# S5's gated result: from a way through DRAM to products of 64x64 blocks with the identity

## The chip, the core and the metric

The kernel runs on one core of one Trainium2 chip. The metric is the device time of one execution in microseconds (us), the median of several runs. TensorE is called PE in the profile, its weight loads PEld, VectorE DVE, ScalarE ACT, GpSimd POOL and SyncE SP. DMA transfers are started from the queues of SP, ACT and POOL.

## What is computed

A layer of an encoder on 512 tokens of 1024 channels, in float32. What matters here is the S5 branch. From the 512 columns `xa` of a projection, seen as 32 groups of 16 channels, it runs a linear recurrence over the tokens forwards and backwards, adds a skip, and passes the sum through gelu. The result y (512 tokens x 512 channels) is multiplied by the sigmoid of its own product with `w_glu`:

```
y = d.reshape(32, 16) * u                      # u: xa as (tokens, 1, 32 groups, 16 channels)
for direction, reverse in ((0, False), (1, True)):
    y = y + s5_scan(u, ..., reverse)
y = gelu(y.reshape(1, tokens, 512))
y = y * sigmoid(y @ w_glu)
```

Beside it runs a gMLP branch. Both are projected (`w_proj_a`, `w_proj_b`), gated, summed and projected by `w_out`; then follow attention over 256 memory tokens and a SwiGLU feed-forward part with a last norm.

## The kernel before, in words

**Large products.** Each float32 weight block is loaded by SP (`wraw`), split into a high part by ScalarE (`whi`, line 85) and a low part by VectorE (`wlo`, line 86), and multiplied in three products of halves (`mm3`, line 350). `feat` gives results with channels on partitions, `tokm` with tokens on partitions. `next_w` keeps the blocks coming: loads are begun three blocks ahead and splits are made two ahead. After each block `tick` runs; it counts time in units of 5.2 us (one `feat` block of 24 products at full width) and calls what was put off by `later(n, fn)` to n such units on. So S5's small steps are laid between the large products.

**Order.** The program is traced in the order of the code, and the library then orders each engine's instructions by a simulated timeline. An instruction may move ahead of others on its engine when its inputs come early. `in_order` (`tc.keep_in_program_order`) pins an instruction behind the one traced last on its engine.

**S5's time axis.** The 512 tokens are 64 chunks (`NCH`) of 8 positions (`Q`). The 32 groups are worked on in four octets (`NO` = 4, `GO` = 8). For octet o, `s5_outputs` does this:

- `ss` is copied out of the states (lines 952, 953).
- `mix_` makes, in one PSUM bank `py`, 24 products of 64 weight columns and 128 moving columns (line 966), in two halves of the array: partitions 0 to 63 and 64 to 127 are the 64 chunks, once for each of two groups, and the free axis is 4 pairs x (8 positions x 16 channels).
- `squash`, at the next tick, applies gelu on ScalarE (line 972) into the first half of the tile `tt`, seen as `yt[:, 0]`.
- `back`, one unit of time after that, turns the four 128x128 blocks by PE transposes into the bank `pyt` (line 978). They are not pinned. Partitions are then (position, channel), the free axis (group, chunk).
- `emit` copies the bank to the second half of `tt` (line 982), and eight transfers of 32 KB, four from SP's queue and four from ScalarE's, write it to the DRAM tile `yd` (line 986), with channels in front.

The octets' input side (`apply`, line 902) makes 16 products of 64 weight columns and 64 moving columns, in two halves of the array, into the bank `pz`; `keep` copies that (line 907). `pump` calls two of them at a time. `products` (lines 818 and 825, bank `pk`) makes the kernels of the octet after next.

**Merge.** When all of S5 is traced, its pool is closed and the pool `merge` opened. Four loads bring `yd` back as `ygt` (line 1174; 128 channels on partitions, m = 0 to 3, the free axis (position, chunk)); each is split into `yg_hi` and `yg_lo`. Then `feat` multiplies by `w_glu`, and `glu_evac` takes the sigmoid and multiplies by `ygt` (line 1183). `w_proj_a` (with the gates `gat`, line 1196) and `w_out` follow.

**The tag "gain".** The pool `norm` has two slots of 4 KB per partition with this tag. They hold, in turn, `g_mix`, `g_row`, `gbr`, `mix`, `g_mem` (the gain of the memory's norm, used at line 498 on `mt`), `g_x` (used there on `h` into `xs`), two tiles of probabilities, `g_f`, `s3`, `pair` and `g_o`. The gains are loaded from SP's queue (line 460). A tile's load waits until the slot's tenant before it has been read.

Of the kernel before, what the change touches and what calls it, by code (L numbers as in the profile page):

```python
# [9 lines left out]
F32 = mybir.dt.float32  # L10
F32R = mybir.dt.float32r
AF = mybir.ActivationFunctionType
ALU = mybir.AluOpType
# [4 lines left out]
P = 128  # L18
D = 1024
T = 512  # L20
# [7 lines left out]
C = 16  # L28
# [11 lines left out]
Q = 8  # L40
NCH = T // Q
NO = 4
GO = G // NO
# [9 lines left out]
def hybrid_layer_kernel(  # L53
# [8 lines left out]
    nc = tc.nc  # L62
# [8 lines left out]
    np_ = ctx.enter_context(tc.tile_pool(name="norm", bufs=2))  # L71
    dp = ctx.enter_context(tc.tile_pool(name="scratch", bufs=1, space=DRAM))
# [4 lines left out]
    def bank(name):  # L77
        return pm.tile([P, 512], F32, tag="mm", name=name)

    def aux(name, shape=(P, 512)):  # L80
        return pa.tile(list(shape), F32, tag="aux", name=name)

    def split(dst_hi, dst_lo, src):

        hi = nc.scalar.copy(dst_hi, src)  # L85
        lo = nc.vector.tensor_tensor(dst_lo, src, dst_hi.bitcast(F32), ALU.subtract)  # L86
        if pinned[0]:
            in_order(hi)
            in_order(lo)
# [3 lines left out]
    in_order = tc.keep_in_program_order  # L93
# [338 lines left out]
    def later(n, fn):  # L432

        side["later"].append((side["now"] + n, fn))
# [28 lines left out]
    ident = cp.tile([P, P], F32, name="ident")  # L463
# [135 lines left out]


    ud = dp.tile([SW, Q, NCH], F32, name="ud")
    yd = [dp.tile([GO * C, Q, NCH], F32, name=f"yd{o}") for o in range(NO)]
    st = {}
    V = nc.vector
    lo_, hi_ = slice(0, 64), slice(64, 128)
# [174 lines left out]
    def lc(t, g):  # L780
        return t[:, g].rearrange("p a b -> p (a b)")
# [160 lines left out]
    def s5_outputs(o):  # L942
        gs = slice(o * GO, (o + 1) * GO)
        while ("oct", o) not in st:
            yield None
        e_re, e_im, tt = st["oct", o]
        zh, u = st["zh"], st["u"]
        ss = s5p.tile([P, 2, GO, NCH], F32, tag="wt", name="ss", bufs=2)
        zv = zh[:, :, :, gs].rearrange("p n i g -> p i g n")
        nc.gpsimd.memset(ss[lo_, :, :, 0:1], 0.0)  # L950
        nc.gpsimd.memset(ss[hi_, :, :, NCH - 1:NCH], 0.0)
        nc.scalar.copy(ss[lo_, :, :, 1:NCH], zv[lo_, :, :, 0:NCH - 1])
        nc.scalar.copy(ss[hi_, :, :, 0:NCH - 1], zv[hi_, :, :, 0:NCH - 1][:, :, :, ::-1])
        ss = (ss[:, 0], ss[:, 1])

        yt = tt.rearrange("p (i r) c -> p i r c", i=2)

        def mix_():
            ps = aux("py", (P, GO // 2, P))
            for r in range(GO // 2):  # L960
                for k in range(3):
                    for j in range(2):
                        g = 2 * r + j
                        a = (u[:, o * GO + g, :], ss[0][:, g, :], ss[1][:, g, :])[k]
                        b = (tt[:, g, :], lc(e_re, g), lc(e_im, g))[k]
                        in_order(nc.tensor.matmul(ps[64 * j:64 * j + 64, r, :], a, b, start=r == k == 0, stop=k == 2,  # L966
                                                  tile_position=(0, 64 * j), skip_group_check=True))
            later(0.5, lambda: squash(ps))

        def squash(ps):  # L970

            nc.scalar.activation(yt[:, 0], ps, AF.Gelu_apprx_tanh)
            later(1, back)

        def back():
            ps = aux("pyt", (P, GO // 2, P))
            for r in range(GO // 2):
                nc.tensor.transpose(ps[:, r, :], yt[:, 0, r, :], ident)
            later(0.5, lambda: emit(ps))

        def emit(ps):
            nc.scalar.copy(yt[:, 1], ps)
            y = yt[:, 1].rearrange("p r (g n) -> p (r g) n", n=NCH)
            ydo = yd[o].rearrange("(g c) l n -> l c g n", c=C)
            for l in range(Q):
                (nc.sync, nc.scalar)[l % 2].dma_start(ydo[l], y[C * l:C * l + C])

        later(0.5, mix_)
        yield 0.1
        yield None  # L990

    def s5_program():
        yield from s5_setup()
        st["zh"] = s5p.tile([P, NCH, 2, G], F32, name="zh")
        later(0.5, pump)
        for n in range(6):
            yield from s5_input(n)
        yield from s5_kernels(0)
        for n in range(6, len(SETS)):
            yield from s5_input(n)  # L1000
        for _ in range(2):
            square_power()
        yield from s5_kernels(1)
        while st.get("nz", 0) < 2 * NO:
            yield None
        yield None
        yield from s5_scan()
        for _ in range(2):
            yield None
        for o in range(NO):  # L1010
            yield from s5_outputs(o)
            if o + 2 < NO:
                yield from s5_kernels(o + 2)
# [114 lines left out]
    for h in range(H):  # L1128
        ps = bank("psv")
# [36 lines left out]
    mgp = mgx.enter_context(tc.tile_pool(name="merge", bufs=1))  # L1166
# [2 lines left out]

    yg_hi = mgp.tile([P, 4, T], F32R, name="yg_hi")  # L1170
    yg_lo = mgp.tile([P, 4, T], F32R, name="yg_lo")
    ygt = mgp.tile([P, 4, T], F32, name="ygt")
    for m in range(4):
        nc.sync.dma_start(ygt[:, m, :], yd[m].rearrange("p l n -> p (l n)"))
        split(yg_hi[:, m, :], yg_lo[:, m, :], ygt[:, m, :])
    ya_hi = mgp.tile([P, 4, T], F32R, name="ya_hi")
    ya_lo = mgp.tile([P, 4, T], F32R, name="ya_lo")

    def glu_evac(m, j, ps):
        z = np_.tile([P, T], F32, tag="ev", name="glu", bufs=2)  # L1180
        nc.scalar.activation(z, ps, AF.Sigmoid)
        z2 = np_.tile([P, NCH, Q], F32, tag="ev", name="glu2", bufs=2)
        nc.vector.tensor_tensor(z2.rearrange("p n l -> p l n"), z.rearrange("p (l n) -> p l n", l=Q),
                                ygt[:, m, :].rearrange("p (l n) -> p l n", l=Q), ALU.mult)
        split(ya_hi[:, m, :], ya_lo[:, m, :], z2.rearrange("p n l -> p (n l)"))

    for c0 in range(0, SW, 256):
        feat(w_glu, c0, (yg_hi, yg_lo), 4, glu_evac)
# [275 lines left out]
    for t0 in (0, 2):  # L1464
        ps = {t: bank(f"pt{t - t0}") for t in (t0, t0 + 1)}
# [77 lines left out]
    ps = [bank("pf0"), bank("pf1")]  # L1543
# [192 lines left out]
    for i in range(2):  # L1736
        p = aux("pcut", (P, 256))
# [37 lines left out]
```

## Time and profile before

| what | value |
|---|---|
| median of 3 runs | 876.34 us |
| lowest and highest run | 876.28 and 878.51 us |
| the profiled execution | 877.18 us |
| its span, first to last instruction | 875.4 us |
| mean granted TensorE clock | 0.997 |
| DMA packets | 112134 |
| moved by DMA | 154.34 MB, 176 GB/s in the mean |

The span is what the engines' instructions cover in the profiled execution; the execution's own time is a little longer. Busy time of PE counts matmuls whose ends are modelled, and matmuls overlap, so prices on PE are read from start to start. A row of a tile or line view gives the count, the shortest, median and longest instruction in ns, and the first and last start in us. In the order of time a row gives start, length, engine, line, operation, result and operands, the used rows and columns of the weights, the moving size, and the count of what was merged into the row.

### The profile page before, as it was taken

The page shows a single profiled execution, that of the slowest core. Times are in us where ns is not written, and L with a number is a line of the kernel's source. Part 1 is how long each engine was busy: PE and PEld are TensorE (multiplying, and loading weights), DVE is VectorE, ACT ScalarE, POOL GpSimd, SP SyncE. Part 2 cuts the span into 40 slices and gives each one's busy share as a digit, 9 for nine tenths or more (in the row PEclk, how much of TensorE's full clock was granted, in tenths as well). Part 3 has the DMA queues.
Part 4 walks back from the last instruction along what each step waited for, and adds up shares of the span by engine and source line. Part 5 has one row for each costly group of instructions (what it writes and reads, how often), then busy time and mean ns, then how long its engine had stood idle before and what let it go on. Part 6 is the DMA issues. An engine that isn't in the chain of part 4 may idle for free.

```text
span 875.4 us, 14560 instructions
## 1 busy us (share of the span) xinstructions
PE 862.9 (99%) x5753; PEld 759.9 (87%) x5753; DVE 617.4 (71%) x867; ACT 464.1 (53%) x684; POOL 104.9 (12%) x154
## 2 busy tenths in 40 slices
PE   9999999999999999999999999999999999999996
PEld 6787888887888888889899878999999999888875
DVE  5699679968313258669657646767877768898875
ACT  5544875277434234557557444645545454556663
POOL 1001065103311100110000001001111110000000
PEclk9999999999999999999999999999999999999998
DMA  8358369943759946825687144547788963256672
GB/s 260 112 148 249 78 200 257 248 125 107 205 133 278 263 134 211 270 88 174 196 262 218 52 137 128 145 129 187 178 217 212 233 165 79 82 166 198 194 249 87
DMA packets 112134, 154.34 MB, mean 176 GB/s; under 512 B 13545, under 2 KB 78593, under 8 KB 112002
## 3 DMA queue, kind: packets, MB, share of 16 engines
q1 hardware_dynamic: 93042, 128.27, 45.2%
q0 software_dynamic: 16432, 24.09, 16.6%
q10 hardware_dynamic: 2592, 1.05, 0.5%
q8 instruction: 45, 0.74, 0.3%
q14 instruction: 23, 0.19, 0.1%
HBM read 146.60 MB, written 38.24 MB: 211 GB/s over the span
## 4 chain that ended last, share of the span: by engine, by line
PE 93%; DVE 5%; ACT 1%; issue 1%; POOL 0%; POOLq 0%
PE pf L350 29%; PE pt L350 17%; PE px L1370 12%; PE dx L350 7%; PE pq L1370 6%; PE dq L350 3%; PE pv L1370 3%; PE qx L1370 2%; PE dv L350 2%; PE ptr L511 1%; PE py L966 1%; PE po L350 1%; PE qq L1370 1%; DVE wlo L86 1%; PE pz L902 1%; PE pw L883 1%
## 5 line engine op out<-in xcount | busy, mean ns | idle before, releaser
L86 DVE TENSOR_TENSOR wlo<-wraw,whi 128x1024 fp32r<-128x1024 f32 (+1 forms) x139 | 165.0, 1187 | 110.2 <-ACT whi L85 106.9
L85 ACT CAST whi<-wraw 128x1024 fp32r<-128x1024 f32 (+1 forms) x139 | 142.3, 1024 | 168.2 <-PE pf L350 60.1
L350 PE MATMUL pf<-xn,whi 128*128 128x512 f32 x448 | 140.6, 393 | 0.0
L350 PEld LDWEIGHTS pf<-xn,whi 128*128 128x128 f32 x448 | 83.4, 188 | 17.9 <-issue 1.1
L350 PE MATMUL pf<-xn,wlo 128*128 128x512 f32 x224 | 87.7, 391 | 0.0
L1370 PE MATMUL px<-fn,whi 128*128 128x256 f32 x480 | 83.3, 277 | 0.0
L1370 PEld LDWEIGHTS px<-fn,whi 128*128 128x128 f32 x480 | 72.4, 188 | 0.3 <-ACT u L1630 0.2
L85 ACT CAST whi<-b 128x1024 fp32r<-128x1024 f32 x40 | 42.1, 1053 | 50.5 <-PE px L1370 27.1
L86 DVE TENSOR_TENSOR wlo<-b,whi 128x1024 fp32r<-128x1024 f32 x40 | 49.0, 1224 | 28.0 <-ACT whi L85 28.0
L1370 PE MATMUL px<-fn,wlo 128*128 128x256 f32 x240 | 66.5, 277 | 0.0
L350 PE MATMUL dx<-whi,s 128*128 128x512 f32 x170 | 53.9, 392 | 1.4 <-ACT whi L85 1.0
L1370 PE MATMUL pq<-s,whi 128*128 128x256 f32 x320 | 55.1, 277 | 0.0
L86 DVE TENSOR_TENSOR wlo<-t,whi 128x1024 fp32r<-128x1024 f32 x30 | 36.7, 1225 | 20.1 <-ACT whi L85 20.1
L85 ACT CAST whi<-t 128x1024 fp32r<-128x1024 f32 x30 | 31.6, 1052 | 36.0 <-PE pv L1370 12.6
L350 PEld LDWEIGHTS pf<-xn,wlo 128*128 128x128 f32 x224 | 42.1, 188 | 8.6
L1370 PEld LDWEIGHTS pq<-s,whi 128*128 128x128 f32 x320 | 48.3, 188 | 0.1
L1370 PEld LDWEIGHTS px<-fn,wlo 128*128 128x128 f32 x240 | 45.1, 188 | 0.0
L1370 PE MATMUL pq<-s,wlo 128*128 128x256 f32 x160 | 44.3, 277 | 0.0
L350 PE MATMUL pt<-whi,xn 128*128 128x512 f32 x128 | 42.4, 404 | 0.0
L350 PEld LDWEIGHTS dx<-whi,s 128*128 128x128 f32 x170 | 31.7, 188 | 8.4 <-ACT whi L85 1.2
L350 PE MATMUL dx<-wlo,s 128*128 128x512 f32 x85 | 33.1, 390 | 0.0
L1370 PEld LDWEIGHTS pq<-s,wlo 128*128 128x128 f32 x160 | 30.1, 188 | 0.0
(436 smaller groups left out, 2132.1 us busy)
## 6 DMA issues: line engine op xcount, KB each, us to landing
wraw<-in_w_in_dram SPq DMA_DIRECT2D x36, 512.0 KB, 5.2
dsum<-in_w_down_dram SPq DMA_DIRECT2D x20, 512.0 KB, 6.9
wraw<-dsum SPq DMA_DIRECT2D x20, 512.0 KB, 4.1
b<-in_w_gate_dram SPq DMA_DIRECT2D x15, 512.0 KB, 4.1
b<-in_w_up_dram SPq DMA_DIRECT2D x15, 512.0 KB, 3.9
wraw<-in_w_down_dram SPq DMA_DIRECT2D x15, 512.0 KB, 3.8
dsum<-in_w_down_dram POOLq DMA_DIRECT2D x10, 512.0 KB, 7.6
dsum<-dsum POOLq DMA_DIRECT2D x10, 512.0 KB, 7.7
```

Source lines behind the costliest of these rows:

```text
L85: hi = nc.scalar.copy(dst_hi, src)
L86: lo = nc.vector.tensor_tensor(dst_lo, src, dst_hi.bitcast(F32), ALU.subtract)
L350: nc.tensor.matmul(ps, a[x], b[y], start=start and i == 0, stop=stop and i == 2, skip_group_check=free)
L511: tr = nc.tensor.transpose(ps[:, j, :], src[:, k * P:(k + 1) * P], ident)
L883: nc.tensor.transpose(ps[:, j, :], wt[:, 4 * hf + j, :], ident)
L902: in_order(nc.tensor.matmul(ps[hf, g, :], wt[:, g, hf], x, start=g == 0, stop=True, tile_position=(0, 64 * j), skip_group_check=True))
L966: in_order(nc.tensor.matmul(ps[64 * j:64 * j + 64, r, :], a, b, start=r == k == 0, stop=k == 2, tile_position=(0, 64 * j), skip_group_chec ...
L1370: nc.tensor.matmul(ps[:, j, :], a[x], b[y], start=start and j == k == i == 0, stop=k == 3 and i == 2, skip_group_check=True)
```

## The change

`mix_` pairs group 4j + r with half j and place r, in place of group 2r + j, so that each half holds four neighbouring groups. `squash` writes gelu's result to the first half of `tt` in another order: `yl`, with the position in front and then (group, channel). Each of its 64x64 blocks (64 chunks on partitions, 64 channels of one position free) is then turned by an ordinary product with the 64x64 identity, in the quarter of the array that belongs to its half: 16 products an octet, pinned by `in_order`. The bank then has 128 channels on partitions and (position, chunk) free, which is the layout of `ygt`. `emit` copies it to one of two tiles `ygt` in the slots "gain", each for two octets. The DRAM tile `yd`, its 32 writes, the four loads and the tile `ygt` of the pool `merge` go away; the splits and `glu_evac` read the new tiles.

```diff
-    yd = [dp.tile([GO * C, Q, NCH], F32, name=f"yd{o}") for o in range(NO)]
+    ygt = []
...
-        yt = tt.rearrange("p (i r) c -> p i r c", i=2)
+        yl = tt[:, 0:GO // 2, :].rearrange("p r (i c) -> p (r i) c", i=2)
...
-                        g = 2 * r + j
+                        g = GO // 2 * j + r
...
-            nc.scalar.activation(yt[:, 0], ps, AF.Gelu_apprx_tanh)
+            nc.scalar.activation(yl.rearrange("p l (r c) -> p r l c", c=C), ps.rearrange("p r (l c) -> p r l c", c=C),
+                                 AF.Gelu_apprx_tanh)
             later(1, back)
 
         def back():
-            ps = aux("pyt", (P, GO // 2, P))
-            for r in range(GO // 2):
-                nc.tensor.transpose(ps[:, r, :], yt[:, 0, r, :], ident)
+
+            ps = aux("pyt", (P, Q, NCH))
+            for l in range(Q):
+                for j in range(2):
+                    hf = slice(64 * j, 64 * j + 64)
+                    in_order(nc.tensor.matmul(ps[hf, l, :], yl[hf, l, :], ident[hf, hf], start=l == 0, stop=True,
+                                              tile_position=(64 * j, 64 * j), skip_group_check=True))
             later(0.5, lambda: emit(ps))
 
         def emit(ps):
-            nc.scalar.copy(yt[:, 1], ps)
-            y = yt[:, 1].rearrange("p r (g n) -> p (r g) n", n=NCH)
-            ydo = yd[o].rearrange("(g c) l n -> l c g n", c=C)
-            for l in range(Q):
-                (nc.sync, nc.scalar)[l % 2].dma_start(ydo[l], y[C * l:C * l + C])
+            if o % 2 == 0:
+                ygt.append(np_.tile([P, 2, T], F32, tag="gain", name="ygt", bufs=2))
+            nc.scalar.copy(ygt[o // 2][:, o % 2, :], ps.rearrange("p l n -> p (l n)"))
...
-    ygt = mgp.tile([P, 4, T], F32, name="ygt")
     for m in range(4):
-        nc.sync.dma_start(ygt[:, m, :], yd[m].rearrange("p l n -> p (l n)"))
-        split(yg_hi[:, m, :], yg_lo[:, m, :], ygt[:, m, :])
+        split(yg_hi[:, m, :], yg_lo[:, m, :], ygt[m // 2][:, m % 2, :])
...
-                                ygt[:, m, :].rearrange("p (l n) -> p l n", l=Q), ALU.mult)
+                                ygt[m // 2][:, m % 2, :].rearrange("p (l n) -> p l n", l=Q), ALU.mult)
```

## The prediction

> **What bounds the kernel now.** I read the page first, parts 1 and 4: busy time by engine, then the chain that ended last.
>
> ```profile
> span 875.4 us, 14560 instructions
> PE 862.9 (99%) x5753; PEld 759.9 (87%) x5753; DVE 617.4 (71%) x867; ACT 464.1 (53%) x684; POOL 104.9 (12%) x154
> ...
> PE 93%; DVE 5%; ACT 1%; issue 1%; POOL 0%; POOLq 0%
> ```
>
> TensorE is busy for 862.9 of 875.4 us and makes 93% of the chain. A 99% average can still hide a stage with another limit, so I ask for the stage of the change alone (the view of windows: length, then PE busy, PEld, DVE, ACT, POOL), and for all waits of PE in the whole kernel (total, count, longest).
>
> ```profile
> 175.00:345.00 170.00, 169.97 (x1010) 139.71 (x1009) 88.20 (x103) 79.85 (x94) 29.48 (x53) 1.00 0.66 181
> ```
> ```profile
> PE pt L350 <- DVE wlo L86: 1.4, 2, 0.7
> PE idle L544 <- DVE dcol L765: 1.1, 1, 1.1
> PE dx L350 <- ACT whi L85: 1.0, 1, 1.0
> PE pt L350 <- ACT ot_hi L85: 0.7, 1, 0.7
> PE ppt L1349 <- DVE prob L1340: 0.6, 1, 0.6
> PE dx L350 <- DVE h L1700: 0.4, 1, 0.4
> ```
>
> From S5's first output product to the end of w_proj_a, PE is idle for 0.03 of 170 us, at granted clock 1.00. Its waits in the whole kernel are 1.4+1.1+1.0+0.7+0.6+0.4 = 5.2 us, and none names yd or ygt. So in this stage an instruction off PE costs nothing while its result comes in time, and every nanosecond that PE gets more or less moves the end.
>
> **Is the way through DRAM hidden?** The views of the tiles yd, ygt and yg_hi (count, min/median/max ns, first and last start):
>
> ```profile
> L986 SPq DMA_DIRECT2D yd<-tt x16: 303/422/443, 205.2 to 264.4; - x16
> L986 ACTq DMA_DIRECT2D yd<-tt x16: 309/441/491, 205.2 to 262.1; - x16
> L1174 SPq DMA_DIRECT2D ygt<-yd x4: 349/586/1874, 266.3 to 269.5; - x4
> L86 DVE TENSOR_TENSOR yg_lo<-ygt,yg_hi x4: 683/693/693, 274.5 to 280.5; 128x512 fp32r<-128x512 f32 x4
> ```
> ```profile
> L350 PE MATMUL pf<-yg_hi,whi x16: 389/389/390, 307.6 to 317.8; 128*128 128x512 f32 x16
> ```
>
> The last half of w_glu's operand is made at 280.5+0.7 = 281.2 us. Its first reader starts at 307.6, because PE is still multiplying by w_proj_b and by the gate's weights. The path has 26 us to spare. What the change removes from it (16 issues of 0.42 us and 4 of 0.59 on SP's queue, 16 of 0.44 on ScalarE's, and the landings) is worth nothing at the end: the cover is those 26 us of other products, and it would have to vanish whole before the path cost a microsecond.
>
> **The change, part by part.** *Removed on PE:* in each of four octets, four 128x128 transposes. One such place in PE's order of time (start, length, instruction):
>
> ```profile
> 200.53 0.39 PE L350 MATMUL pf<-xn,wlo 128*128 128x512 f32 x1
> 200.76 0.60 PE L978 MATMUL pyt<-ident,tt 128*128 128x128 f32 x4
> 201.12 0.70 PE L350 MATMUL pf<-xn,whi 128*128 128x512 f32 x2
> 201.65 0.39 PE L350 MATMUL pf<-xn,wlo 128*128 128x512 f32 x1
> ```
>
> I price from start to start, since matmuls overlap. The transposes begin 0.23 us after the product ahead, which is that product's own step (0.22 and 0.23 in the rows here and below; I take 0.227), so entering is free. They hold PE from 200.76 to 201.12 = 0.36 us, and the two products behind take 0.53 in place of 0.455: 0.075 to leave. Together 0.44 us an octet, 1.74 in four.
>
> *Added on PE:* in each octet 8 blocks x 2 halves = 16 ordinary f32 products, weights 64x64, 64 columns, each half in its own quarter of the array. No row has that form. The nearest is S5's input product (L902): also 64 columns of weights, 64 columns moving, two halves of the array side by side, but 128 rows deep.
>
> ```profile
> 111.92 0.39 PE L350 MATMUL pf<-xn,wlo 128*128 128x512 f32 x1
> 112.14 0.39 PE L350 MATMUL pf<-xn,whi 128*128 128x512 f32 x1
> 112.46 2.08 PE L902 MATMUL pz<-u,ex 128*64 128x64 f32 x64
> 114.48 0.27 PE L1087 MATMUL prs<-ident,rs 128*8 128x128 f32 x1
> 114.51 0.48 PE L350 MATMUL pf<-xn,whi 128*128 128x512 f32 x1
> 114.82 0.40 PE L350 MATMUL pf<-xn,wlo 128*128 128x512 f32 x1
> ```
>
> An f32 product is two records there (two sets of 16 products, `pump` takes two at once, give x64). So 32 products take 114.48-112.46 = 2.02 us, 16 take 1.01, a pair of halves 0.126. Entering costs 112.46-112.14-0.227 = 0.09, leaving 114.82-114.51-0.227 = 0.08. An octet: 1.01+0.17 = 1.18 us; four: 4.72.
>
> Bounds of this unknown. Above: the two quarters do not overlap, and 16 products take 2.02 us, with the switch 2.19 an octet; nothing in the trace excludes it, as no product there splits the rows. Below: no switch at all and 16 products at the row's rate, 1.01; were the pairs also to reach the rate of S5's output product per column (L966, 24 products of 128 columns from 207.75 to 210.52 us, so 2.77/12/2 = 0.115 a pair of 64 columns), 0.92. I take 1.18, the nearest row.
>
> ```profile
> 207.45 0.28 PE L825 MATMUL pk<-e,bd 128*16 128x16 f32 x16
> 207.75 0.44 PE L966 MATMUL py<-tt,u 128*64 128x128 f32 x4
> ...
> 210.52 0.72 PE L350 MATMUL pf<-xn,whi 128*128 128x512 f32 x2
> ```
>
> **Sum:** 4.72-1.74 = +2.98 us on a PE that never waits here. The bounds give 4x0.92-1.74 = +1.9 and 4x2.19-1.74 = +7.0.
>
> The Trainium skill, "TensorE: Matmul & The Clock Gate", section "Back-to-back issue gap", puts a floor of about 25 ns under a matmul of up to 64 columns; as an estimate, 32 records an octet would be 0.8 us, which with the switch gives +2.1. The row shows 2.02 us/64 = 31.6 ns, and I stay with the row.
>
> *Order.* The transposes were free to move; the new products are `in_order`, behind everything traced before them on PE. `squash` is traced one tick (24 products) after `mix_`, and `back` one more, so 48 x 0.227 = 10.9 us behind the mixing products, not 24 products as at 200.76. A pinned product that waits would stop all of PE behind it. It waits for the gelu on ScalarE:
>
> ```profile
> L972 ACT ACTIVATE tt<-py x4: 592/598/598, 199.0 to 254.5; 128x512 f32<-128x512 f32 x4
> L982 ACT COPY tt<-pyt x4: 578/583/586, 204.6 to 260.1; 128x512 f32<-128x512 f32 x4
> L907 ACT COPY zh<-pz x8: 1060/1098/1137, 92.4 to 114.6; 128x512 f32<-128x512 f32 x8
> ```
>
> The last gelu starts at 254.5, the copy behind the last transposes at 260.1, and the products would come some 5.5 us (24 x 0.227) behind where the transposes stood, about 265: ten microseconds of cover. The gelu now writes runs of 16 values apart from each other. Its price lies between 0.60 and the 1.10 us of L907, which writes single values apart; ScalarE is busy for 80 of 170 us, so either costs nothing. The final copy keeps its size. Cost: zero. The octet after next loads into the same tile, now free when PE has read it and not when a transfer has. The row below is the first load of octet 3; octet 1's products come near 210.5+10.9 = 221.4, long before. Cost: zero.
>
> ```profile
> 238.87 0.56 POOL L851 DMA_DIRECT2D tt<-kd  x1 [0.87 <-PE pf L350]
> ```
>
> *The slots of ygt.* The result now lives in the two "gain" slots, so g_mem and g_x wait on SP's queue until w_glu's evacuation has read it.
>
> ```profile
> L460 SPq DMA_DIRECT2D g_x<-in_xattn_norm_g_dram x1: 333/333/333, 160.6 to 160.6; - x1
> L498 DVE SCALAR_TENSOR_TENSOR xs<-h,r,g_x x8: 742/746/753, 380.6 to 396.9; 128x512 f32<-128x512 f32 x8
> ```
> ```profile
> L460 SPq DMA_DIRECT2D g_mem<-in_mem_norm_g_dram x1: 333/333/333, 135.8 to 135.8; - x1
> L498 DVE SCALAR_TENSOR_TENSOR mt<-mt,r,g_mem x4: 743/749/752, 352.5 to 365.6; 128x512 f32<-128x512 f32 x4
> L1183 DVE TENSOR_TENSOR glu<-glu,ygt x4: 1127/1142/1165, 311.1 to 321.5; 128x512 f32<-128x512 f32 x4
> ```
>
> The first slot falls free after the second of L1183's four, about 316, the other at 321.5+1.1 = 322.6. Behind a waiting g_mem or g_x on SP stand w_out's loads, and behind those the casts and w_out's products from 340. Loads run several blocks ahead, g_mem is first read at 352.5 and g_x at 380.6, so 30 us are left for a transfer; cost zero. If that cover were gone, each microsecond for which SP is held past w_out's due time would be one of PE.
>
> **The forecast.** The profiled execution took 877.18 us (span 875.4 and 1.8 around it), 0.84 above the median of 876.34, within the three runs' 876.28 to 878.51. 877.18+2.98 = 880.2 for a like execution, 879.3 for the median. About 0.3% (2.6 us) is what a measurement of this kernel can tell from no change; this forecast is 0.34%, just beyond it.
>
> **Rivals.** *The products are cheap, and it is not measurably slower.* The place: `back` of octets 0 and 1 falls in the tick in which pk and py, also in part-array modes, run (about 207 and 221 us), so the switch is shared, two times 0.17; and the shallower quarters stream at 0.92. Then 4x0.92+2x0.17-1.74 = +2.3: 878.6. It decides where an octet falls under 0.44+2.63/4 = 1.10 us. For it: 1.18 is only 0.08 above. Against it: pk to py takes 0.30 us from start to start, so two modes that follow each other pay for the switch as well.
>
> *The quarters take turns.* +7.0: 883.3. For it: both halves write one PSUM bank, and no row shows it done from different rows. Against it: the two halves of L902 write one bank too and overlap.
>
> The Trainium skill, "TensorEngine Tiling (Array Packing)", section "Restrictions and Gotchas", says that different row tiles cannot access the same PSUM bank at once, and leaves the order to software. By that rule this rival would be the result; no run so far shows row tiles.
>
> *Another order of the queues.* The kernel's instructions are ordered by a simulated timeline, and 36 transfers less, with two weights loaded late, shift it. PE's 5.2 us of waits could go, 879.3-5.2 = 874.1, or as many appear, 884.5. Against it: asked by stage, the waits on wlo and dcol all lie ahead of 100 us and the other four behind 480, far from S5.
>
> *The way through DRAM did matter*, and its end shows: excluded by the 26 us, no chance of its own.
>
> **How the numbers follow.** Forecast 0.50; as its own spread is near 0.8 us, 0.38 of it beyond +0.3% and 0.12 within. Cheap products 0.27, within. Taking turns 0.09, slower. Another order 0.14: 0.05 faster, 0.04 within, 0.05 slower. So faster 0.05, within 0.43, slower 0.52. The range reaches from 876.0 (cheap products, 878.6, with half of the waits, 2.6, gone) to 883.3 (taking turns); for the likeliest case alone it is 878.2 to 880.6.
>
> **What would show it.** pyt as 128 records of a 64-column form in place of 16, an octet's start-to-start near 1.18 us (1.01 and the switches), PE's busy time up by about 3 us with its waits unchanged; yg_lo done before 275 us and w_glu's first product at 307.6+3; g_mem and g_x issued near 316 and 323, and no wait of PE between 175 and 400. An octet of 2.2 us is the turn-taking. A wait of PE on gelu, or on wlo of w_out, would make the prediction wrong, as would a total that falls although pyt grows.

## The result, and the profile after

The changed kernel takes 882.15 us in the median (879.84 to 884.00, 7 runs), the kernel before 876.98 us beside it (876.04 to 879.25, 7 runs). The ratio is 1.0049, with a 95% interval of 1.0031 to 1.0068: slower by 2.7 to 6.0 us. The profiled execution of the changed kernel is the one of 882.15 us. Beside the first four experiments below the kernel before ran 23 times; one of these runs took 4933.59 us and is left out of their ratios.

The page of the changed kernel, parts 1 and 4, the lines that answer to those of before:

```profile
span 880.3 us, 14705 instructions
PE 864.2 (98%) x5865; PEld 761.0 (86%) x5865; DVE 617.5 (70%) x867; ACT 464.2 (53%) x684; POOL 105.0 (12%) x154
...
PE 89%; DVE 5%; DMA 2%; issue 1%; ACT 1%; SPq 1%; POOLq 0%; POOL 0%; DVEq 0%; ACTq 0%
```

The span grew by 4.9 us and PE's busy time by only 1.3. Such totals mix stages, so I cut both spans at two marks that both kernels have: the first product of `psv` (before S5's outputs begin) and the first product of `qx` (behind `w_out`). The marks in the order of time, before and then after:

```profile
152.13 1.05 PE L1131 MATMUL psv<-wsx,zt 128*128 128x128 f32 x8
...
433.88 0.41 PE L1370 MATMUL qx<-hn,whi 128*128 128x256 f32 x2
```
```profile
152.59 0.60 PE L1134 MATMUL psv<-wsx,zt 128*128 128x128 f32 x4
...
438.38 0.41 PE L1371 MATMUL qx<-hn,whi 128*128 128x256 f32 x2
```

The view of windows between these marks (window, length, then PE busy, PEld, DVE, ACT, POOL), before and then after:

```profile
0.00:152.13 152.13, 149.45 (x1025) 120.64 (x1026) 118.50 (x243) 88.59 (x160) 35.76 (x57) 1.00 0.66 186
152.13:433.88 281.75, 281.72 (x1649) 237.58 (x1648) 173.50 (x231) 136.67 (x184) 39.95 (x67) 1.00 0.66 188
433.88:875.40 441.52, 431.69 (x3082) 401.69 (x3080) 325.39 (x395) 238.85 (x341) 29.22 (x30) 0.99 0.59 166
```
```profile
0.00:152.59 152.59, 147.68 (x1025) 119.79 (x1025) 118.29 (x242) 89.06 (x160) 36.26 (x58) 0.99 0.68 182
152.59:438.38 285.79, 284.70 (x1762) 239.79 (x1760) 173.71 (x232) 136.39 (x184) 39.31 (x66) 1.00 0.64 180
438.38:880.30 441.92, 431.79 (x3082) 401.40 (x3080) 325.47 (x395) 238.80 (x341) 29.38 (x30) 1.00 0.59 165
```

The middle rows are the stage of the change. It is 285.79-281.75 = 4.04 us longer: PE is busy for 284.70-281.72 = **2.98 us** more, and idle for 1.09 us in place of 0.03, which is **1.06 us** of waiting. The rest of the span's 4.90 us is 0.46 ahead of the stage and 0.40 behind it. PE's waits in that stage; the kernel before has none there:

```profile
PE pk L818 <- DVE e L807: 1.1, 1, 1.1
```

This one wait stands at octet 0. The order of time of PE there, and at octet 2, where nothing waits, in the changed kernel:

```profile
200.99 0.39 PE L350 MATMUL pf<-xn,wlo 128*128 128x512 f32 x1
201.31 1.15 PE L982 MATMUL pyt<-ident,tt 64*64 64x64 f32 x32
203.55 0.43 PE L818 MATMUL pk<-e,bd 128*32 128x128 f32 x8 [1.09 <-DVE e L807]
203.91 0.72 PE L350 MATMUL pf<-xn,whi 128*128 128x512 f32 x2
```
```profile
240.96 0.39 PE L350 MATMUL pf<-yb_hi,wlo 128*128 128x512 f32 x1
241.28 1.15 PE L982 MATMUL pyt<-ident,tt 64*64 64x64 f32 x32
242.36 0.73 PE L350 MATMUL pf<-xn,whi 128*128 128x512 f32 x2
242.93 0.40 PE L350 MATMUL pf<-xn,wlo 128*128 128x512 f32 x1
```

An octet by itself (241.28): 241.28-240.96-0.227 = 0.09 to enter, 242.36-241.28 = 1.08 of products, 242.93-242.36-0.455 = 0.11 to leave, together 1.28 us. At octet 0 the kernel products of the octet after next (`pk`, line 818) come straight behind the turning products and could start near 203.55-1.09 = 202.46. They wait for VectorE, whose row comes first here; then the same VectorE step before, and PE there:

```profile
202.27 1.22 DVE L807 TENSOR_TENSOR e<-e,etmp 128x1024 f32<-128x1024 f32 x1
```
```profile
201.81 1.23 DVE L807 TENSOR_TENSOR e<-e,etmp 128x1024 f32<-128x1024 f32 x1
```
```profile
203.72 0.39 PE L350 MATMUL pf<-xn,wlo 128*128 128x512 f32 x1
204.04 0.42 PE L818 MATMUL pk<-e,bd 128*32 128x128 f32 x8
```

VectorE keeps the same schedule: 202.27-152.59 and 201.81-152.13 are both 49.68 us after the stage's mark. Before, twelve large products stood between the transposes and `pk`, which started 1.0 us after VectorE had ended (201.81+1.23 = 203.04). After, `pk` has moved up behind the turning products and is ready before its operand.

The way through DRAM, its end, and the gains that now come late, in the tile view (count, min/median/max ns, first and last start):

```profile
L86 DVE TENSOR_TENSOR yg_lo<-ygt,yg_hi x4: 684/686/694, 262.6 to 264.5; 128x512 fp32r<-128x512 f32 x4
...
L350 PE MATMUL pf<-yg_hi,whi x16: 389/389/389, 312.1 to 322.3; 128*128 128x512 f32 x16
```
```profile
L460 SPq DMA_DIRECT2D g_mem<-in_mem_norm_g_dram x1: 557/557/557, 321.0 to 321.0; - x1
...
L498 DVE SCALAR_TENSOR_TENSOR mt<-mt,r,g_mem x4: 745/750/754, 357.1 to 370.1; 128x512 f32<-128x512 f32 x4
```

`yg_lo` is done at 265.2 in place of 281.2 us, and its reader does not start a moment sooner: 312.1 in place of 307.6, later by what PE lost ahead of it. `g_mem` is issued at 321.0 and used at 357.1.

### The profile page after: what moved, and what is told of

Read it like the earlier page. It is cut to its first block, busy times and chain, and to the rows that moved or that the text cites. A ratio compares the mean times of both kernels' runs of the same rounds, so it can differ in the third digit from the quotient of the medians.

```text
span 880.3 us, 14705 instructions
## 1 busy us (share of the span) xinstructions
PE 864.2 (98%) x5865; PEld 761.0 (86%) x5865; DVE 617.5 (70%) x867; ACT 464.2 (53%) x684; POOL 105.0 (12%) x154
## 4 chain that ended last, share of the span: by engine, by line
PE 89%; DVE 5%; DMA 2%; issue 1%; ACT 1%; SPq 1%; POOLq 0%; POOL 0%; DVEq 0%; ACTq 0%
PE pf L350 27%; PE pt L350 16%; PE px L1371 12%; PE dx L350 6%; PE pq L1371 6%; PE dq L350 3%; PE pv L1371 3%; PE qx L1371 2%; PE dv L350 2%; DMA xt<-in_x_dram 1%; PE po L350 1%; PE qq L1371 1%; PE ptr L511 1%; DVE wlo L86 1%; PE py L966 1%
## 5 line engine op out<-in xcount | busy, mean ns | idle before, releaser
L350 PEld LDWEIGHTS pt<-whi,xn 128*128 128x128 f32 x128 | 24.3, 194 | 6.7 <-ACT xn L85 1.8
```

Of the source, the lines that this page charges most:

```text
L350: nc.tensor.matmul(ps, a[x], b[y], start=start and i == 0, stop=stop and i == 2, skip_group_check=free)
```

## The experiments

Two theories stood against each other. **A:** the stage pays on PE alone, 2.98 us for the products and 1.1 for the wait of `pk`, which follows from its place in the order. **B:** the queues, the slots of `ygt` or the late gains play a part. The stage between the marks is compared, since the start of the kernel differs from run to run (below). Its rows in the view of windows, one kernel a fence, stand with each experiment. Each time is a median, and each ratio is to runs of the kernel before made beside it (medians 877.57 us for the first four experiments, 877.66 for the others), with its 95% interval.

**`pk` one unit of time later.**

```diff
-        later(1, products)
+        later(2 if o > 1 else 1, products)
```

> The changed kernel, but the kernels of octets 2 and 3 (products, lines 818 and 825) are called one unit of time later, so that they do not stand straight behind the turning products. Theory A: of the change's 4.9 us of span, 3.0 are the price of the 64 products against 16 transposes, 1.1 a wait of PE at pk for VectorE's line 807 that came with the new order, and the rest is the start. Then the wait goes and the time is 1.1 us below the changed kernel's, about +3.4 us over the kernel before. Theory B: the queues' other order (two gains loaded late, transfers gone) costs the rest, and the wait only stands in for it: the time stays at +4.5 or above, or the wait appears at another place.

881.23 us (880.19 to 881.61), ratio 1.0041 [1.0026, 1.0055]. The stage in the view of windows, and PE's waits in it:

```profile
151.99:436.66 284.67, 284.29 (x1761) 239.89 (x1760) 173.53 (x231) 136.53 (x184) 39.38 (x66) 1.00 0.64 179
```
```profile
PE pk L818 <- DVE e L809: 0.4, 1, 0.4
```

The stage is 1.12 us shorter than that of the changed kernel: the wait on L807 is gone, one of 0.4 us on the next VectorE step came, and PE is busy for 0.41 us less. In the order of time at octet 0 the mixing products now follow the turning products, so one switch serves both:

```profile
200.71 1.15 PE L982 MATMUL pyt<-ident,tt 64*64 64x64 f32 x32
201.79 0.44 PE L966 MATMUL py<-tt,u 128*64 128x128 f32 x4
```

So the wait on L807 hangs on the place of `pk`, as A says. That the stage came out 1.1 us shorter, as expected, is luck in part: of the wait 0.4 us came back at the next products of `pk` (B's sign of a wait at another place, though again one of `pk` on VectorE), and the shared switches made up for it. The whole times, 881.23 and 882.15 us, are too near each other to tell the two kernels apart.

**The turning products free to move.**

```diff
-                    in_order(nc.tensor.matmul(ps[hf, l, :], yl[hf, l, :], ident[hf, hf], start=l == 0, stop=True,
-                                              tile_position=(64 * j, 64 * j), skip_group_check=True))
+                    nc.tensor.matmul(ps[hf, l, :], yl[hf, l, :], ident[hf, hf], start=True, stop=True,
+                                     tile_position=(64 * j, 64 * j), skip_group_check=True)
```

> The changed kernel with its turning products not pinned in program order; each starts its own accumulation, as a transpose does. Theory A: the price of the products stays (1.08 us an octet from start to start), so +3 us at least; the wait at pk goes only if the order changes by it. If the pin itself is the cause of the wait, the time is 1.1 us below the changed kernel's. If the pin is not the cause, pk stands behind the products again and waits about 1 us.

881.58 us (880.16 to 882.59), ratio 1.0047 [1.0031, 1.0063]. The stage, and octet 0 in the order of time:

```profile
150.91:436.70 285.79, 284.70 (x1762) 239.77 (x1761) 173.43 (x231) 136.46 (x184) 39.34 (x66) 1.00 0.64 180
```
```profile
199.64 1.15 PE L982 MATMUL pyt<-ident,tt 64*64 64x64 f32 x32
201.87 0.43 PE L818 MATMUL pk<-e,bd 128*32 128x128 f32 x8 [1.09 <-DVE e L807]
```

The same stage and the same wait to the hundredth. The pin has no part in it.

**No turn, direct.** The changed kernel without the 16 products; the copy reads gelu's result.

```diff
-            ps = aux("pyt", (P, Q, NCH))
-            for l in range(Q):
...
+            ps = yl
```

> The changed kernel without the turning products: the copy to ygt reads gelu's result itself, so the blocks are not turned (this part of the computation is left out). No way through DRAM, no work on PE for the turn. Theory A: the time of the kernel before minus its transposes, 4 x 0.44 = 1.8 us below it, and equal to the next run within the spread, since the way through DRAM is hidden. Theory B, if the late gains and the other order of the queues cost something: above the next run by 1 us or more. If the way through DRAM did matter: below the next run by 1 us or more.

**No turn, through DRAM.** The kernel before without the transposes, and all its transfers kept.

```diff
-            ps = aux("pyt", (P, GO // 2, P))
-            for r in range(GO // 2):
-                nc.tensor.transpose(ps[:, r, :], yt[:, 0, r, :], ident)
+            ps = yt[:, 0]
```

> The kernel before without its transposes: the copy ahead of the transfers reads gelu's result itself (the turn is left out), and the way through DRAM stays, 32 writes and 4 loads. Theory A: 1.8 us below the kernel before, and within 1 us of the run before this one. The difference of the two is what the way through DRAM and the tile's place in the slots are worth with PE's work alike.

Direct: 876.47 us (874.49 to 878.84), ratio 0.9984 [0.9969, 0.9999]. Through DRAM: 875.39 us (873.62 to 876.94), ratio 0.9975 [0.9965, 0.9986]. The stages in the view of windows, direct and then through DRAM:

```profile
151.24:431.12 279.88, 279.85 (x1633) 235.89 (x1632) 173.31 (x231) 136.69 (x184) 39.83 (x67) 1.00 0.65 184
```
```profile
152.18:432.03 279.85, 279.85 (x1633) 235.89 (x1632) 173.37 (x231) 136.34 (x184) 39.54 (x67) 1.00 0.67 190
```

These two differ in the whole of the change but the turn: 36 transfers, the slots, the late gains. PE is busy for the same 279.85 us, and the stages are 0.03 us apart. B falls for this stage: nothing beside the turn is worth anything in it. For the rest of the kernel B is not excluded. The median of the direct kernel is 1.08 us above the other's, which reaches the 1 us named as B's sign. The two profiled executions, with spans of 873.5 and 873.6 us, do not show where: ahead of the stage the direct one is 0.94 us shorter, behind it 0.81 longer, and only some 0.25 us of that, at the very end, comes again in every kernel without the way through DRAM (last section). The version with true transposes below speaks against more: it goes the direct way too, its stage is 0.68 us longer than that of the kernel before, and its median only 0.08 us above. The pair prices the turns, too, by taking them away: 281.72-279.85 = 1.87 us for the transposes, 284.70-279.85 = 4.85 for the new products, a difference of 2.98.

**The products twice.**

```diff
-            for l in range(Q):
+            for l in (*range(Q), *range(Q)):
```

> The changed kernel with every turning product issued twice (the second writes the same values again): 64 products more, nothing else. Theory A, that PE's work is the price: 16 more products hold PE 0.94 us (16 steps of 58.5 ns a pair of records, from the changed kernel's profile), so +3.7 us over the changed kernel from first large product to last, whatever the order; about +7 us or 0.8% over the kernel before with the wait at pk, which may shrink, since 0.94 us more lie ahead of pk. If other engines set the pace there, less than +2.

885.38 us (884.16 to 887.14), ratio 1.0088 [1.0067, 1.0108]. The stage, and octet 0 in the order of time, with the two waits that follow it:

```profile
152.12:442.18 290.06, 288.30 (x1890) 243.61 (x1888) 173.41 (x231) 133.81 (x182) 39.39 (x66) 1.00 0.63 177
```
```profile
200.84 2.08 PE L982 MATMUL pyt<-ident,tt 64*64 64x64 f32 x64
203.09 0.43 PE L818 MATMUL pk<-e,bd 128*32 128x128 f32 x8 [0.17 <-DVE e L807]
...
205.61 0.43 PE L818 MATMUL pk<-e,bd 128*32 128x128 f32 x8 [1.20 <-DVE e L809]
```

Octet 1, where no wait follows directly:

```profile
214.62 2.08 PE L982 MATMUL pyt<-ident,tt 64*64 64x64 f32 x64
216.63 0.43 PE L818 MATMUL pk<-e,bd 128*32 128x128 f32 x8
```

From start to start 32 products take 216.63-214.62 = 2.01 us, and 16 take 1.08 at the same place in the changed kernel (217.69 to 218.77, below). So sixteen more products cost 0.93 us, and 1.08-0.93 = 0.15 us of a group does not grow with its length. Four times 0.93 is 3.72; PE's busy time grows by 288.30-284.70 = 3.60 us, a little less, as the mixing products here follow octet 2's turning products directly, at 245.44 us, and share a switch with them. So 4.85-3.72 = 1.13 of the 4.85 us is what stands around the products: the switches and that fixed part. The wait on L807 shrinks, since the added products fill most of it, but 1.20 and 0.40 us on L809 come in its place. Waits here trade places with work in front of them; PE's busy time is what can be added up.

**Columns split, rows not.** All 128 rows of weights in each half, with the identity's other half multiplying zeros.

```diff
-                    in_order(nc.tensor.matmul(ps[hf, l, :], yl[hf, l, :], ident[hf, hf], start=l == 0, stop=True,
-                                              tile_position=(64 * j, 64 * j), skip_group_check=True))
+                    in_order(nc.tensor.matmul(ps[hf, l, :], yl[:, l, :], ident[:, hf], start=l == 0, stop=True,
+                                              tile_position=(0, 64 * j), skip_group_check=True))
```

> The changed kernel, but each turning product takes all 128 partitions of the block and 64 columns of the 128x128 identity, so only the array's columns are split (the form of line 902) and not its rows. The result is the same. If splitting the rows costs or saves nothing, an octet takes what it takes in the changed kernel, 1.08 us from start to start, and the time is that of the changed kernel. If quarters of the array are dearer (both write one bank from different rows), this is faster by up to 1 us; if they are cheaper, slower.

881.06 us (880.40 to 882.65), ratio 1.0037 [1.0021, 1.0053]. The stage, and octet 2 in the order of time:

```profile
153.47:439.24 285.77, 284.67 (x1762) 239.80 (x1761) 173.50 (x231) 136.50 (x184) 39.32 (x66) 1.00 0.64 180
```
```profile
241.82 0.39 PE L350 MATMUL pf<-yb_hi,wlo 128*128 128x512 f32 x1
242.14 1.15 PE L982 MATMUL pyt<-ident,tt 128*64 128x64 f32 x32
243.22 0.73 PE L350 MATMUL pf<-xn,whi 128*128 128x512 f32 x2
```

243.22-242.14 = 1.08 us, as with quarters. Here two quarters of the array that write one bank from different rows cost no more and no less than two halves of its columns.

**True transposes into the same layout.** Each half of the mixing products gets four positions of all eight groups in place of all positions of four groups: 48 products of 64 moving columns. Then four 128x128 transposes give `w_glu`'s layout, and the copy goes straight to `ygt`.

```diff
-            for r in range(GO // 2):
+            for g in range(GO):
                 for k in range(3):
                     for j in range(2):
-                        g = GO // 2 * j + r
+                        cs = slice(64 * j, 64 * j + 64)
...
-                        b = (tt[:, g, :], lc(e_re, g), lc(e_im, g))[k]
+                        b = (tt[:, g, cs], lc(e_re, g)[:, cs], lc(e_im, g)[:, cs])[k]
...
+            for l in range(Q // 2):
+                nc.tensor.transpose(ps[:, l, :], yl[:, l, :], ident)
```

> A version that keeps true transposes without the way through DRAM: mix_ gives each half of the array four positions of all eight groups (48 products of 64 moving columns an octet in place of 24 of 128), so gelu's result can be turned by four 128x128 transposes straight into w_glu's layout; they are not pinned. By the rows: 24 pairs x 0.126 = 3.02 us for the mixing in place of 2.77, and 0.44 for the turn as in the kernel before, so +1.0 us over the kernel before and 2 to 3 below the changed kernel, when no new wait comes. If writing runs of 16 columns to PSUM is slow, the mixing takes longer than 3.3 us an octet and the gain is lost.

877.74 us (876.52 to 879.80), ratio 1.0004 [0.9993, 1.0015]. The stage, and the transposes of octet 3 in the order of time:

```profile
153.11:435.54 282.43, 282.43 (x1842) 238.69 (x1841) 173.59 (x231) 136.00 (x184) 39.60 (x67) 1.00 0.65 182
```
```profile
257.54 0.60 PE L980 MATMUL pyt<-ident,tt 128*128 128x128 f32 x4
257.89 0.47 PE L350 MATMUL pf<-yb_hi,wlo 128*128 128x512 f32 x1
```

The transposes cost 0.35 us again, PE never waits, and the stage is 0.68 us longer than before. The mixing products have it: from the first of them to the next large product, here and then before (octet 2),

```profile
230.87 0.34 PE L966 MATMUL py<-tt,u 128*64 128x64 f32 x4
...
233.82 0.50 PE L350 MATMUL pf<-yb_lo,whi 128*128 128x512 f32 x1
```
```profile
234.11 0.44 PE L966 MATMUL py<-tt,u 128*64 128x128 f32 x4
...
236.88 0.50 PE L350 MATMUL pf<-yb_hi,whi 128*128 128x512 f32 x1
```

2.95 against 2.77 us, four times 0.18 = 0.72. So the way through DRAM can be left out at almost no price, and, as the pair without the turn says, at no gain: this kernel cannot be told from the one before.

**The kernel before again**, for the spread of one program.

> The kernel before once more, for its profile alone. If the 0.5 us by which the changed kernel's profile is behind ahead of S5's outputs is the start's own spread, the time at which the first psv product starts (152.1 us in the first profile, 150.9 to 152.6 in the five others) differs here as well, by up to 1 us. If it belongs to the change, it is 152.1 again.

876.73 us. The stage in the view of windows:

```profile
151.67:433.40 281.73, 281.72 (x1650) 237.49 (x1649) 173.71 (x231) 136.80 (x184) 39.49 (x66) 1.00 0.67 187
```

The stage repeats to 0.02 us, PE's busy time in it to 0.01. What lies ahead of it does not: the mark came at 151.67 and at 152.13 us in two executions of one program, and between 150.91 and 153.47 in the ten profiles.

## Why the prediction was right, and where it was not

- **PE bounds the stage, so PE's price is the stage's price:** right. Every difference of a stage above is PE's busy time plus a wait of PE.
- **The way through DRAM is hidden and worth nothing:** right, by the pair without the turn.
- **Products against transposes, +2.98 us:** measured 2.98, and the agreement to the hundredth is luck. The products were put at 4.72 and measured 4.85, the transposes at 1.74 and measured 1.87: both 0.13 too low, and the errors cancel. An octet by itself takes 1.28 us and not 1.18: 1.08 in place of 1.01 for the products, 0.20 in place of 0.17 for the switches. The prediction's row was the right one, 2.02 us for 32 products against 2.01 of the new form, but it was halved for 16, and the fixed 0.15 us does not halve: a pair of halves costs 2x0.93/16 = 0.116 us and not 0.126. In octets 0 and 1 `pk` follows the turning products directly, so that one switch serves both; octet 1 in the changed kernel:

```profile
217.69 1.15 PE L982 MATMUL pyt<-ident,tt 64*64 64x64 f32 x32
218.77 0.42 PE L818 MATMUL pk<-e,bd 128*32 128x128 f32 x8
```

  The rival of cheap products named that sharing for these octets; it is real: these two octets come to (4.85-2x1.28)/2 = 1.15 us each in the mean, and the 1.28 of the other two more than use up the gain.
- **The quarters take turns, +7.0:** fallen, by the split of columns alone. The Trainium skill, "TensorEngine Tiling (Array Packing)", section "Restrictions and Gotchas", says that different row tiles cannot access the same PSUM bank at once. Here sixteen products in two row tiles that write one bank took 1.08 us, the time that products without row tiles need, so for this form no turn-taking shows and the measurement decides. Whether both halves wrote in the same instant no row can say.
- **"*Order* … Cost: zero":** this is the step that failed. It put the turning products 48 large products behind the mixing products; they ran 24 behind, where the transposes had run (201.31 against 200.76): harmless. It asked only whether the pinned product itself would wait, for gelu. What waited was the instruction behind it, `pk`, on VectorE, for 1.06 us. The rival "another order of the queues" had named this mechanism with 5.2 us either way; it came at a fifth of that, beside the forecast and not in its place.
- **The slots of `ygt`, cost zero:** right. The gains come late, and PE has no wait for them in the stage.
- **The sum:** forecast was +0.34%, measured 0.49%, with the forecast inside the interval. The span was forecast at 875.4+2.98 = 878.4 us and came at 880.3. The 1.9 us between are the wait (1.06), the start (0.46, within the spread of one program) and the end (0.40, of which some 0.2 comes again in every kernel without the way through DRAM). The median of 882.15 us lies in the range of 876.0 to 883.3 but outside the 878.2 to 880.6 given for the likeliest case alone, which had no new wait in it.
- **"PE's busy time up by about 3 us with its waits unchanged":** true of the stage for the busy time, false for the waits. The total rose by only 1.3, because PE's busy time ahead of the stage, which the change does not touch, came out 1.8 lower in this execution; in the second execution of the kernel before it was 147.02 us, 2.4 lower.

What stays open: why the ordered program puts `pk` directly behind the turning products. That the library's simulated timeline prices them otherwise than the transposes is a thought, not shown; shown is only that the pin is not the reason, and that tracing `pk` later takes the wait on L807 away. Open, too, is what the direct way costs outside the stage: 1.08 us between the medians of the two kernels without the turn, of which the profiles place a quarter of a microsecond at the end.

## What to carry to other kernels

On a saturated engine, price a way around it by what it does to that engine: here 36 transfers that 26 us of other products cover are worth nothing in their stage, and 4.85 us of products in place of 1.87 of transposes are paid in full. Where a scheduler orders the instructions, check not only the edited instruction for new waits but its neighbours: look up how long each operand of the instruction behind it had been ready in the profile before, and treat slack of the size that was lost here, a microsecond, as at risk. Compare stages between marks on the bounding engine, and not whole times, when the difference is of the size of the spread.

## What the runs showed that was not expected

- Depth costs nothing here: an f32 product of 64 moving columns takes the same 1.08 us in sixteen with 64 or 128 rows of weights.
- To enter the products on part of the array costs 0.09 us and to leave them 0.11, even where only 1.08 us of work lies between: 16% of the octet. The price of leaving is not that of the split alone: behind the transposes on the whole array, which cost nothing to enter, it is 0.075 to 0.09 (octet 1 of the kernel before: 216.33-216.01-0.227).
- From the last product of `pcut` to the end of the span pass about 7.4 us in the three profiles of kernels with the way through DRAM (875.4-867.99 in the kernel before), and about 7.7 in the seven without it (880.3-872.67 = 7.6 to 877.2-869.50 = 7.7). The difference lies behind the issue of the last output transfer, 3.9 to 4.0 us ahead of the end in the three and 4.2 to 4.3 in the seven. Its cause was not looked for.
